# Attention stage: negated logits, second weight parts on VectorE, closer spacing of heads and top-key rounds

## The chip, the cores and the metric

The kernel runs on one core of a Trainium2 chip. A core has TensorE (matmuls and transposes), VectorE, ScalarE and GpSimd (elementwise work), and SyncE, which issues most loads. In the profile they are PE (PEld for its weight loads), DVE, ACT, POOL and SP. The metric is the device time of one execution in microseconds; a kernel's time is the median of its runs.

## The reference, cut to what matters

Two transformer blocks run one after the other on 512 tokens of width 1024. The change lies in the attention of the second block, which has two branches of eight heads (64 wide, two key and value heads each). In the first branch an indexer scores all causal keys, and each query keeps its 128 best (`topk = min(256, 512 // 4)`); the softmax runs over these. In the second branch a query sees a window of 128 keys, and a learned number per head, the sink, joins the softmax's denominator.

```python
# first branch, per block of 128 queries
score = einsum('bqhk,bqh->bqk', relu(s), wb);  score = where(causal, score, -inf)
_, sel = lax.top_k(score, topk)
logits = einsum('bqgrd,bqkgd->bqgrk', qg, ks) * scale
p = softmax(where(valid, logits, -inf));  o = einsum('bqgrk,bqkgd->bqgrd', p, vs)
# second branch, blocks of 128 queries x 256 keys
logits = where(mask, einsum('bnqgrd,bnkgd->bngrqk', qb, kb) * HEAD_DIM ** -0.5, -inf)
p = softmax(concatenate([logits, sink], -1))[..., :-1]
o = einsum('bngrqk,bnkgd->bnqgrd', p, vb)
# both: mix = sigmoid(g_a) * (o_a @ w_branch_a) + sigmoid(g_b) * (o_b @ w_branch_b)
```

## The kernel before

Activations stay in SBUF, weights stream from memory. Each fp32 factor of a dense product is held as a first part (rounded, `hi`) and a second part (the rest, `lo`), and `mm` (line 243) issues three matmuls per block: first x first, first x second, second x first. The stream (`Stream`, line 187) works on a fixed list of units (`plan`). For a unit of up to 128x1024 numbers SyncE loads the raw weights (line 197, three raw buffers), ScalarE writes the first part (line 220, `advance`) and another engine subtracts to get the second part (line 208, `flush`). That engine is `W.eng`, VectorE by default; three units (`ON_POOL`) are always GpSimd's. Before the change line 1165 sets `W.eng` to GpSimd ahead of the projection of the second branch's queries, and line 1253 sets it back behind `w_out_2`. `advance` runs on about every half tick and first flushes the second parts of the first parts issued earlier; each flush also issues the loads that now have a buffer (`pump`).

Everything that is not dense work is written as generators, woven into the dense matmuls by a counter (`Weave`, line 61). A tick is one dense unit of eight K blocks and 128 output features; a projection calls the counter at quarter or half ticks, and a task that yields 0.75 goes on 0.75 ticks later. The order thus made is the program order of every engine's queue, and each engine executes its queue in order. `finish` (line 100) turns the counter with no dense work in between, until the named tasks are done.

In the stage of the change the dense projections come in this order: indexer queries and keys, `bq`, `bk` (second branch), `aq` (4 ticks), `ak` (2), the gate of the second branch (8, line 1204), the branch projection `w_branch_b_2` (4), the gate of the first branch (8, line 1216), `w_branch_a_2` (line 1236), `w_out_2`. Woven into them are: the indexer (line 1015), then 16 rounds of top-key search for each of three query blocks (`top_keys`, line 1035, one round each `TOP_EVERY` ticks), which overwrite the kept scores and make a mask of them; 16 pairs of sliding-window heads, one started each `SWA_EVERY` ticks (line 1176), finished by line 1205; and 16 pairs of first-branch heads, one each `ATT_EVERY` ticks (line 1207), finished by line 1217, where a query block starts only when its keys are known.

One pair of heads (`attend`, line 1045) runs thus: TensorE makes logits (line 1012); VectorE adds the mask and takes the row maximum in one instruction (line 1065), joins the sink (`mx`, line 1068, second branch only) and negates (`nm`, line 1070); ScalarE exponentiates with `nm` as bias and sums (line 1073). Half a tick later VectorE adds the sink's share (`sums`, line 1081) and takes reciprocals (1083), ScalarE scales the weights (1085); 0.75 ticks later TensorE transposes them (1094) and ScalarE copies them out (1096); 0.75 ticks later TensorE multiplies with the values (1103). At the end of each gate ScalarE copies the last block and applies the sigmoid to four blocks at once (line 1200), with a table load of its own. In the branch projection behind the first branch, line 1226 multiplies on VectorE, line 1227 adds on GpSimd, and `split` (line 145) makes the parts `mh` on ScalarE and `ml` on VectorE (line 148).

Of the kernel before, what the change touches and what calls it, by code (L numbers as in the profile page):

```python
# [7 lines left out]
F32 = mybir.dt.float32  # L8
F32R = mybir.dt.float32r
AF = mybir.ActivationFunctionType  # L10
ALU = mybir.AluOpType
# [3 lines left out]
P = 128  # L15
# [6 lines left out]
NEG = -3.0e38  # L22
CUT = -3.2e38
GONE = -3.4e38
MASKED = -1.0e30
NB_RAW = 3
NB_SPLIT = 5
LEAD = 3
LAG_N, LAG_T, LAG_V, LAG_Q, LAG_S = 0.5, 0.75, 0.75, 1, 0.5
SPREAD_Q = 0.25  # L30
SWA_EVERY = 0.75
ON_POOL = (0, 228, 229)
RET_LAG, RET_EVERY = 1, 2
TOP_EVERY = 0.45
ATT_EVERY = 0.7

COLS = [
    ("sgu_ln_g", 8), ("sgu_ln_b", 8),
# [22 lines left out]
class Weave:  # L61
# [13 lines left out]
    def run(self, gen):  # L75

        t = self.spawn(gen)
        self._step(t)
        if not self.inside:
            t["cd"] += self.cur  # L80
        return t
# [26 lines left out]
def tile_kernel(  # L108
# [7 lines left out]
    nc = tc.nc  # L116
    ctx.enter_context(tc.manual_schedule())
    const = ctx.enter_context(tc.tile_pool(name="const", bufs=1))
# [11 lines left out]
    def bigt(shape, name, dt=F32):  # L130
        return big.tile(shape, dt, tag="big", name=name)
# [4 lines left out]
    def tmp2(shape, name, dt=F32):  # L136
        return tp2.tile(shape, dt, tag="t2", name=name)
# [4 lines left out]
    def sm(w, name):  # L142
        return small.tile([P, 16], F32, tag="sm", name=name)[:, :w]
# [93 lines left out]
    W = Stream()  # L237
# [155 lines left out]
    run = wv.run  # L393
# [26 lines left out]
    sinkb = const.tile([P, 8], F32, name="sinkb")  # L420
# [299 lines left out]
    for c in range(2):  # L720
        dense_b(b_units(w_in, 1024 + c * 512), hT,
                lambda t, q, c=c: nc.scalar.activation(
                    v[t // 2][:, t % 2, c * 512:(c + 1) * 512], q, AF.Copy))
# [210 lines left out]
    nc.gpsimd.memset(band, 0.0)  # L934
    nc.gpsimd.affine_select(band, band, [[-1, 256]], ALU.is_ge, MASKED, 128, 1)
    nc.gpsimd.affine_select(band, band, [[1, 256]], ALU.is_gt, MASKED, 0, -1)

    wk_t = bigt([P, 2048], "work")
    work = wk_t[:, 0:1152]
    vb = wk_t[:, 1152:1664].rearrange("p (t c) -> p t c", t=NT)  # L940
# [12 lines left out]
    def q_rope(q, t, name, dst, scale, h0=0):  # L953
        n = 4 * len(dst)
        if (name, t // 2) not in parts:
            parts[name, t // 2] = bigt([P, 2, 8, 2, 64], "hl", F32R)
        hl = parts[name, t // 2][:, t % 2, h0:h0 + n]
        tb = tmp2([P, n, 2, 32], "rq2")
        cos, sin = cs(t)
        rope(q, tb, n, 32, cos, sin)  # L960
        tb = tb.rearrange("p h s c -> p h (s c)")
        yield LAG_S
        split(hl[:, :, 0, :], hl[:, :, 1, :], tb)
        yield LAG_Q + SPREAD_Q * t
        for i, d in enumerate(dst):
            q2 = ps()
            transposes(q2, hl[:, i * 4:i * 4 + 4].bitcast(F32).rearrange("p h s c -> p (h s c)"), 4)
            nc.scalar.activation(
                d[:, :, t * P:(t + 1) * P], q2.rearrange("p (a b) -> p a b", a=4), AF.Copy, scale=scale)
# [65 lines left out]
    def top_keys(t):  # L1035
        wk = work[:, woff[t]:woff[t] + (t + 1) * P]
        for rnd in range(16):
            m8 = sm(8, "m8")
            nc.vector.max(m8, wk)
            nc.vector.match_replace(wk, m8, wk, GONE)  # L1040
            yield TOP_EVERY
        nc.vector.tensor_scalar(wk, wk, CUT, MASKED, op0=ALU.is_gt, op1=ALU.mult)
        kept.add(t)

    def attend(br, t, j, put):

        g = j // 2
        qT, kT = ((aqT, akT), (bqT, bkT))[br]
        k0 = 0 if br == 0 else max(0, t - 1)
        nk = t + 1 - k0  # L1050
        n = nk * P
        if br == 0:
            mask = band[:, P:] if t == 0 else work[:, woff[t]:woff[t] + n]
        else:
            mask = band[:, 256 - n:]
        if n > 256:
            pr = [tmp2([P, T], "pr") for _ in range(2)]
        else:
            pp_ = tmp2([P, 2, 256], "pr")
            pr = [pp_[:, i, :] for i in range(2)]  # L1060
        mx = sm(2, "mx")
        for i in range(2):
            q = ps()
            scores(q, qT, 2 * j + i, t, (kT[0][:, g], kT[1][:, g]), k0 * P, n)
            nc.vector.tensor_tensor_reduce(
                pr[i][:, :n], q[:, :n], mask, 1.0, -3.0e38, ALU.add, ALU.max, mx[:, i:i + 1])
        if br == 1:
            nc.vector.tensor_tensor(mx, mx, sinkb[:, 2 * j:2 * j + 2], ALU.max)
        nm = sm(2, "nm")
        nc.vector.tensor_scalar(nm, mx, -1.0, None, op0=ALU.mult)  # L1070
        sums = sm(2, "sums")
        for i in range(2):
            nc.scalar.activation(pr[i][:, :n], pr[i][:, :n], AF.Exp, bias=nm[:, i:i + 1],  # L1073
                                 accum_out=sums[:, i:i + 1])
        if br == 1:
            es = sm(2, "es")
            nc.vector.tensor_tensor(es, sinkb[:, 2 * j:2 * j + 2], nm, ALU.add)
            nc.scalar.activation(es, es, AF.Exp)
        yield LAG_N
        if br == 1:  # L1080
            nc.vector.tensor_tensor(sums, sums, es, ALU.add)  # L1081
        rs = sm(2, "rs")
        nc.vector.reciprocal(rs, sums)
        for i in range(2):
            nc.scalar.activation(pr[i][:, :n], pr[i][:, :n], AF.Copy, scale=rs[:, i:i + 1])
        yield LAG_T
        pT = {}
        for b0 in range(0, nk, 2):
            nb = min(2, nk - b0)
            q = ps()  # L1090
            for b in range(nb):
                for i in range(2):
                    s = (b * 2 + i) * P
                    nc.tensor.transpose(q[:, s:s + P], pr[i][:, (b0 + b) * P:(b0 + b + 1) * P], ident)  # L1094
            o = tmp2([P, 2, 2, P], "pT")
            nc.scalar.activation(o[:, :nb].rearrange("p b i t -> p (b i t)"), q[:, :nb * 2 * P], AF.Copy)
            for b in range(nb):
                pT[b0 + b] = o[:, b]
        yield LAG_V
        q = ps()  # L1100
        for b in range(nk):
            for i in range(2):
                nc.tensor.matmul(q[i * 64:(i + 1) * 64, :P], vab[br][:, k0 + b, g * 64:(g + 1) * 64],  # L1103
                                 pT[b][:, i, :], start=(b == 0), stop=(b == nk - 1))
        put(j, t * P, (t + 1) * P, q[:, :P])
# [21 lines left out]
    done = {"iq": [], "ik": [], "bq": [], "bk": [], "aq": [], "ak": []}  # L1127
# [22 lines left out]
    bqT = q_tiles("bqT")  # L1150
# [5 lines left out]
    def index_all():  # L1156
# [4 lines left out]
        for t in range(1, NT):  # L1161
            yield from top_keys(t)

    idx_task = wv.spawn(index_all())
    W.eng = nc.gpsimd
    dense_bs([(b_units(w_in_2, 1352),
               lambda t, q: done["bq"].append(run(q_rope(q, t, "bq", bqT, 0.125))))],
             hT2, [(0, 1), (2, 3)])
    dense_bs([(b_units(w_in_2, 1864, 256),
               lambda t, q: done["bk"].append(run(kv(q, t, bkT, vab[1]))))],  # L1170
# [1 line left out]
    aqT = q_tiles("aqT")  # L1172
    akT = k_tiles(gpool, "g", "akT")
    wv.finish(done["bk"])
    ob = Branch()
    swa = wv.spawn(stagger(
        [attend(1, t, j, lambda j, a, b, q: split(ob.hi[:, j, a:b], ob.lo[:, j, a:b], q))
         for j in range(4) for t in range(NT)], SWA_EVERY))
    dense_bs([(b_units(w_in_2, 0),
               lambda t, q: done["aq"].append(run(q_rope(q, t, "aq", aqT, 0.125))))],  # L1180
             hT2, [(0, 1), (2, 3)])
    dense_bs([(b_units(w_in_2, 512, 256),
               lambda t, q: done["ak"].append(run(kv(q, t, akT, vab[0]))))],
# [66 lines left out]
            norms.append(run(norm_T(t, xrow(t), g_mlp, h3T)))  # L1250

    down(w_out_2, KD, mix_pair, fin)
    W.eng = nc.vector

    u2 = []

# [81 lines left out]
```

## Time and profile before

| | before |
|---|---|
| median of 3 runs | 1616.56 us (1616.42 to 1617.55) |
| profiled execution, its own time | 1612.59 us |
| its span, first to last instruction | 1610.8 us |
| TensorE busy, mean granted clock | 98%, 0.994 |
| VectorE, ScalarE, GpSimd busy | 47%, 38%, 20% |

The page gives busy time and a chain of waits for the whole span; TensorE is 82% of the chain. The page's slices show where VectorE is fullest: between about 890 and 1130 us, the stage described above, its tenths are 7 and 8, against 2 to 6 nearly everywhere else. The stage is then read in windows and in the timeline. A wait in the waits view names the instruction that ended it, which may itself have waited for another. A group's mean duration contains any time in which the instruction had been started but was held.

### The profile page before, as it was taken

The page shows a single profiled execution, that of the slowest core. Times are in us where ns is not written, and L with a number is a line of the kernel's source. Part 1 is how long each engine was busy: PE and PEld are TensorE (multiplying, and loading weights), DVE is VectorE, ACT ScalarE, POOL GpSimd, SP SyncE. Part 2 cuts the span into 40 slices and gives each one's busy share as a digit, 9 for nine tenths or more (in the row PEclk, how much of TensorE's full clock was granted, in tenths as well). Part 3 has the DMA queues.
Part 4 walks back from the last instruction along what each step waited for, and adds up shares of the span by engine and source line. Part 5 has one row for each costly group of instructions (what it writes and reads, how often), then busy time and mean ns, then how long its engine had stood idle before and what let it go on. Part 6 is the DMA issues. An engine that isn't in the chain of part 4 may idle for free.

```text
span 1610.8 us, 19774 instructions
## 1 busy us (share of the span) xinstructions
PE 1577.0 (98%) x7844; PEld 1320.0 (82%) x7844; DVE 763.1 (47%) x1309; ACT 613.3 (38%) x1012; POOL 329.8 (20%) x300
## 2 busy tenths in 40 slices
PE   9999999999999999999998999999999999999998
PEld 8888888888888888888887888777877988878886
DVE  4247323453546544455336788778443322233333
ACT  5232223322324433334324456665833323233222
POOL 1015000341004122111005444232345211010000
PEclk9999999999999999999999999999999999999999
DMA  6332333212441233334331421222133333232221
GB/s 204 98 92 71 100 105 92 79 53 90 146 129 55 82 102 92 104 91 146 105 95 49 143 61 49 76 69 76 53 131 92 92 105 103 82 119 96 99 92 52
DMA packets 187247, 151.75 MB, mean 94 GB/s; under 512 B 5218, under 2 KB 157410, under 8 KB 186644
## 3 DMA queue, kind: packets, MB, share of 16 engines
q1 hardware_dynamic: 185072, 144.01, 29.8%
q0 software_dynamic: 1504, 5.44, 1.0%
q8 instruction: 61, 1.00, 0.2%
q10 hardware_dynamic: 580, 1.05, 0.2%
q14 instruction: 30, 0.25, 0.0%
HBM read 146.29 MB, written 4.19 MB: 93 GB/s over the span
## 4 chain that ended last, share of the span: by engine, by line
PE 82%; DVE 8%; ACT 4%; POOL 2%; issue 2%; DMA 0%; POOLq 0%; DVEq 0%; ACTq 0%
PE ps L246 25%; PE ps L247 25%; PE ps L245 25%; PE ps L279 1%; ACT pr L1073 1%; DVE work L1029 1%; PE ps L1012 1%; PE ps L1103 1%; PE ps L1094 1%; PE ps L772 1%; POOL Ya L1227 1%; DVE sums L1081 1%; ACT wh L220 1%; POOL rstd L460 1%; PE ps L487 1%
## 5 line engine op out<-in xcount | busy, mean ns | idle before, releaser
L220 ACT ACTIVATE wh<-wr 128x1024 fp32r<-128x1024 f32 (+1 forms) x259 | 270.9, 1051 | 251.3 <-PE ps L247 119.2
L208 DVE TENSOR_TENSOR wl<-wr,wh 128x1024 fp32r<-128x1024 f32 (+1 forms) x212 | 257.6, 1226 | 172.3 <-ACT wh L220 172.3
L245 PE MATMUL ps<-wh,ls 128*128 128x512 f32 x432 | 168.4, 390 | 1.2 <-ACT ls L147 1.2
L247 PE MATMUL ps<-wh,ls 128*128 128x512 f32 x432 | 168.2, 389 | 0.3 <-DVE ls L148 0.3
L246 PE MATMUL ps<-wl,ls 128*128 128x512 f32 x432 | 168.1, 389 | 0.0
L208 POOL TENSOR_TENSOR wl<-wr,wh 128x1024 fp32r<-128x1024 f32 x47 | 114.5, 2444 | 134.9 <-ACT wh L220 134.8
L245 PE MATMUL ps<-h2Th,wh 128*128 128x512 f32 (+1 forms) x352 | 133.5, 379 | 0.0
L246 PE MATMUL ps<-h2Tl,wh 128*128 128x512 f32 (+1 forms) x352 | 133.5, 379 | 0.0
L247 PE MATMUL ps<-h2Th,wl 128*128 128x512 f32 (+1 forms) x352 | 133.5, 379 | 0.0
L245 PE MATMUL ps<-hTh,wh 128*128 128x512 f32 (+1 forms) x256 | 97.7, 382 | 0.0
L247 PE MATMUL ps<-hTh,wl 128*128 128x512 f32 (+1 forms) x256 | 96.4, 376 | 0.0
L246 PE MATMUL ps<-hTl,wh 128*128 128x512 f32 (+1 forms) x256 | 96.2, 376 | 0.0
L245 PEld LDWEIGHTS ps<-wh,ls 128*128 128x128 f32 x432 | 81.1, 188 | 18.5 <-ACT ls L147 1.6
L245 PE MATMUL ps<-h3Th,wh 128*128 128x512 f32 (+1 forms) x256 | 96.2, 376 | 0.0
L246 PE MATMUL ps<-h3Tl,wh 128*128 128x512 f32 (+1 forms) x256 | 96.2, 376 | 0.0
L247 PE MATMUL ps<-h3Th,wl 128*128 128x512 f32 (+1 forms) x256 | 96.2, 376 | 0.0
L247 PEld LDWEIGHTS ps<-wh,ls 128*128 128x128 f32 x432 | 81.1, 188 | 17.6 <-DVE ls L148 0.8
L246 PEld LDWEIGHTS ps<-wl,ls 128*128 128x128 f32 x432 | 81.1, 188 | 16.7
L896 ACT ACTIVATE hid<-ps,cols 128x512 f32<-128x512 f32 x44 | 34.3, 780 | 144.8 <-PE ps L247 144.8
L897 DVE SCALAR_TENSOR_TENSOR hid<-ps,cols,hid 128x511 f32<-128x511 f32 x44 | 33.0, 749 | 116.8 <-ACT hid L896 116.8
L904 POOL TENSOR_TENSOR act<-hid 128x512 f32<-128x512 f32 x22 | 45.2, 2055 | 194.1 <-DVE hid L899 180.1
L246 PEld LDWEIGHTS ps<-h2Tl,wh 128*128 128x128 f32 x352 | 66.2, 188 | 12.5
(312 smaller groups left out, 3283.4 us busy)
## 6 DMA issues: line engine op xcount, KB each, us to landing
wr<-in_w_in_dram SPq DMA_DIRECT2D x86, 512.0 KB, 3.8
wr<-in_w_up_dram SPq DMA_DIRECT2D x76, 512.0 KB, 3.9
wr<-in_w_down_dram SPq DMA_DIRECT2D x54, 512.0 KB, 3.7
wr<-in_w_out_dram SPq DMA_DIRECT2D x16, 512.0 KB, 3.9
wr<-in_w_sgu_o_dram SPq DMA_DIRECT2D x8, 512.0 KB, 4.2
wr<-in_w_ret_o_dram SPq DMA_DIRECT2D x8, 512.0 KB, 4.3
g<-in_rows_dram POOLq DMA_DIRECT2D x6, 512.0 KB, 7.2
x<-in_x_dram SPq DMA_DIRECT2D x4, 512.0 KB, 5.7
```

The lines of the kernel that those rows point to most:

```text
L208: eng.tensor_tensor(lo, self.raw.pop(i), hi.bitcast(F32), ALU.subtract)
L220: nc.scalar.activation(hi, self.raw[self.n_hi], AF.Copy)
L245: nc.tensor.matmul(q, lhs[0], rhs[0], start=start, stop=False)
L246: nc.tensor.matmul(q, lhs[0], rhs[1], start=False, stop=False)
L247: nc.tensor.matmul(q, lhs[1], rhs[0], start=False, stop=stop)
L279: nc.tensor.matmul(q[:, :256], wslice(u, k, 0, P)[i], act.at(k, 0, 256)[j], start=(i + j + k == 0), stop=(i == 1 and k == K - 1))
L460: nc.gpsimd.tensor_tensor(r, r, nhalf, ALU.pow)
L487: nc.tensor.transpose(q[:, i * P:(i + 1) * P], xn[:, k * P:(k + 1) * P], ident)
L772: nc.tensor.matmul(o, kz[:, d, c - d, :], vc[c], start=True, stop=True)
L896: nc.scalar.activation(o, q, AF.Identity, bias=col("conv_b", f), scale=col("conv_w1", f))
L897: nc.vector.scalar_tensor_tensor(o[:, 1:], q[:, :T - 1], col("conv_w0", f), o[:, 1:], ALU.mult, ALU.add)
L904: nc.gpsimd.tensor_tensor(act[fa // 4][:, fa % 4, :], a, b, ALU.mult)
```

## The change

The logits are made negative: the query copies carry -0.125 in place of 0.125, masked places get +1e30 in place of -1e30, the fused instruction takes the minimum in place of the maximum, and the exponential gets a scale of -1. What was `nm` (minus the maximum) is then the minimum itself, so the negation per pair of heads is left out; the sink joins by a minimum with a negated copy, `nsink`, made once. The two lines that hand the second parts of the weights to GpSimd in this stage and back are left out, so VectorE makes them. Three spacings become smaller.

```diff
-MASKED = -1.0e30
+MASKED = 1.0e30
...
-SWA_EVERY = 0.75
+SWA_EVERY = 0.65
...
-TOP_EVERY = 0.45
-ATT_EVERY = 0.7
+TOP_EVERY = 0.38
+ATT_EVERY = 0.6
...
+    nsink = const.tile([P, 8], F32, name="nsink")
+    nc.vector.tensor_scalar(nsink, sinkb, -1.0, None, op0=ALU.mult)
...
-        mx = sm(2, "mx")
+        nm = sm(2, "nm")
...
             nc.vector.tensor_tensor_reduce(
-                pr[i][:, :n], q[:, :n], mask, 1.0, -3.0e38, ALU.add, ALU.max, mx[:, i:i + 1])
+                pr[i][:, :n], q[:, :n], mask, 1.0, 3.0e38, ALU.add, ALU.min, nm[:, i:i + 1])
         if br == 1:
-            nc.vector.tensor_tensor(mx, mx, sinkb[:, 2 * j:2 * j + 2], ALU.max)
-        nm = sm(2, "nm")
-        nc.vector.tensor_scalar(nm, mx, -1.0, None, op0=ALU.mult)
+            nc.vector.tensor_tensor(nm, nm, nsink[:, 2 * j:2 * j + 2], ALU.min)
         sums = sm(2, "sums")
         for i in range(2):
-            nc.scalar.activation(pr[i][:, :n], pr[i][:, :n], AF.Exp, bias=nm[:, i:i + 1],
+            nc.scalar.activation(pr[i][:, :n], pr[i][:, :n], AF.Exp, bias=nm[:, i:i + 1], scale=-1.0,
                                  accum_out=sums[:, i:i + 1])
...
-    W.eng = nc.gpsimd
     dense_bs([(b_units(w_in_2, 1352),
-               lambda t, q: done["bq"].append(run(q_rope(q, t, "bq", bqT, 0.125))))],
+               lambda t, q: done["bq"].append(run(q_rope(q, t, "bq", bqT, -0.125))))],
...
-               lambda t, q: done["aq"].append(run(q_rope(q, t, "aq", aqT, 0.125))))],
+               lambda t, q: done["aq"].append(run(q_rope(q, t, "aq", aqT, -0.125))))],
...
     down(w_out_2, KD, mix_pair, fin)
-    W.eng = nc.vector
```

## Rows read from the trace of the kernel before

**Rows 1.** Waits of TensorE, 880 to 1215 us: total, times, longest.

```profile
PE ps L1094 <- ACT pr L1085: 3.8, 3, 3.1
PE ps L1103 <- ACT pT L1096: 3.5, 3, 2.3
PE ps L493 <- ACT pT L1096: 2.2, 1, 2.2
PE ps L246 <- POOL wl L208: 1.8, 1, 1.8
PE ps L493 <- DVE hl L148: 0.8, 1, 0.8
```

**Rows 2.** Busy us by stretch: PE, PEld, DVE, ACT, POOL, granted clock, DMA, GB/s.

```profile
950.00:970.00 20.00, 16.81 (x83) 13.51 (x82) 16.05 (x44) 14.17 (x34) 4.50 (x4) 0.95 0.16 46
970.00:990.00 20.00, 20.00 (x117) 16.11 (x116) 17.59 (x50) 11.89 (x35) 9.09 (x6) 0.97 0.24 57
1170.00:1190.00 20.00, 17.39 (x76) 13.69 (x75) 7.48 (x10) 7.46 (x11) 5.72 (x4) 0.83 0.47 169
1210.00:1240.00 30.00, 28.19 (x121) 22.90 (x120) 7.32 (x8) 9.80 (x12) 17.98 (x10) 0.94 0.42 123
```

**Rows 3.** Groups of VectorE and GpSimd, 880 to 1215 us: busy, mean ns, idle.

```profile
L1070 DVE TENSOR_SCALAR nm<-mx 128x2 f32<-128x2 f32 x32 | 19.1, 596 | 1.1
L1081 DVE TENSOR_TENSOR sums<-sums,es 128x2 f32<-128x2 f32 x16 | 11.3, 704 | 0.0
L1068 DVE TENSOR_TENSOR mx<-mx,sinkb 128x2 f32<-128x2 f32 x16 | 5.5, 346 | 0.6
L148 DVE TENSOR_TENSOR ml<-Ya,mh 128x512 fp32r<-128x512 f32 x8 | 11.6, 1445 | 16.5 <-ACT mh L147 16.5
...
L208 POOL TENSOR_TENSOR wl<-wr,wh 128x1024 fp32r<-128x1024 f32 x37 | 89.7, 2429 | 132.0 <-ACT wh L220 132.0
```

**Rows 4.** The page, costliest groups: the second parts that VectorE makes.

```profile
L208 DVE TENSOR_TENSOR wl<-wr,wh 128x1024 fp32r<-128x1024 f32 (+1 forms) x212 | 257.6, 1226 | 172.3 <-ACT wh L220 172.3
```

**Rows 5.** Timeline, GpSimd and VectorE: a long nm and a plain one.

```profile
1002.38 4.72 POOL L208 TENSOR_TENSOR wl<-wr,wh 128x1024 fp32r<-128x1024 f32 x2
...
1004.83 2.31 DVE L1070 TENSOR_SCALAR nm<-mx 128x2 f32<-128x2 f32 x1
...
1057.21 0.17 DVE L1070 TENSOR_SCALAR nm<-mx 128x2 f32<-128x2 f32 x1
```

**Rows 6.** Timeline around the first sliding-window head: GpSimd, VectorE, TensorE.

```profile
961.57 2.40 POOL L208 TENSOR_TENSOR wl<-wr,wh 128x1024 fp32r<-128x1024 f32 x1 [10.18 <-ACT wh L220]
...
962.01 3.37 DVE L1029 SCALAR_TENSOR_TENSOR work<-relu,work 128x512 f32<-128x512 f32 x2 [2.27 <-ACT relu L1023]
...
968.02 0.77 PE L1094 MATMUL ps<-ident,pr 128*128 128x128 f32 x2 [3.06 <-ACT pr L1085]
```

**Rows 7.** Timeline at the end of the last gate projection: TensorE, ScalarE.

```profile
1168.17 1.09 PE L1103 MATMUL ps<-pT,va 128*64 128x128 f32 x16
1169.20 1.09 PE L1094 MATMUL ps<-ident,pr 128*128 128x128 f32 x8
...
1174.54 0.80 PE L245 MATMUL ps<-obh,wh 128*128 128x512 f32 x1
...
1170.19 1.91 ACT L1200 ACTIVATE Ya<-Ya 128x2048 f32<-128x2048 f32 x1
```

**Rows 8.** Timeline of the branch projection: ml plain and long, and TensorE.

```profile
1191.19 0.69 DVE L148 TENSOR_TENSOR ml<-Ya,mh 128x512 fp32r<-128x512 f32 x1 [2.06 <-ACT mh L147]
...
1210.99 2.18 DVE L148 TENSOR_TENSOR ml<-Ya,mh 128x512 fp32r<-128x512 f32 x1 [2.06 <-ACT mh L147]
...
1212.67 0.50 PE L246 MATMUL ps<-wl,mh 128*128 128x512 f32 x1 [1.81 <-POOL wl L208]
```

**Rows 9.** Timeline of GpSimd where VectorE still makes the second parts.

```profile
899.44 0.86 POOL L510 TENSOR_TENSOR rq<-rope 128x256 f32<-128x256 f32 x1 [2.83 <-DVE rope L504]
900.57 1.57 POOL L510 TENSOR_TENSOR rq<-rope 128x256 f32<-128x256 f32 x1 [0.28 <-DVE rope L504]
```

## The prediction

> **What bounds it now.** I read the page's first two parts, then TensorE's waits, then the windows with the clock, then VectorE's groups with their mean durations, and last the timeline around each wait. TensorE is busy for 98% of the span, so only the time in which it stands or runs at the lower clock can be won; the change leaves its matmuls as they are. In the stretch of the change (880 to 1215 us) the waits view lists few idle stretches [rows 1]: 3.8 us of softmax transposes on the scaled weights, 3.5 us of value matmuls on the transposed weights (2.3 of it one wait at the very end), 2.2 us of key transposes, 1.8 us on a second part made by GpSimd, 0.8 us on a rotated query: 12.1 us in all. After the longer ones the granted clock falls to its lower level for a while; one minus the granted clock, times the window, gives 1.0 and 0.6 us after the first head, 3.4 us at the end of attention, 1.8 us in the projection behind it [rows 2]: 6.8 us. So 18.9 us, 1.2%, is about what can be had. Gaps too short for the waits view come on top.
>
> Who makes TensorE wait is seen one step back. VectorE's `nm`, on two numbers per partition, takes 0.17 us when left alone [rows 5] and 596 ns on average; `sums` averages 704 ns and `mx` 346 ns [rows 3]. In the timeline an `nm` begins at 1004.83 and ends at 1007.14, just when a pair of GpSimd's second parts ends (1002.38 plus 4.72) [rows 5]. So a small VectorE operation that falls on one of GpSimd's 37 second parts (2429 ns each [rows 3]) is held until that ends, and behind it stand the exponential on ScalarE, the reciprocal, the scaling and the transposes.
>
> **Part 1: second parts from GpSimd to VectorE.** Off GpSimd go 37 x 2.43 = 90 us; VectorE gains 37 x 1.226 = 45.4 us [rows 3, 4]. It loses the holds: 32 x (596 - 170) ns = 13.6 us on `nm`, 16 x (704 - 170) = 8.5 on `sums`, 16 x (346 - 170) = 2.8 on `mx`, 8 x (1445 - 690) = 6.0 on `ml` [rows 3, 5, 8], 30.9 us. With part 2 (5.4 us) that is 36.3 against 45.4: VectorE gets up to 9 us more work, nearer none because other lines, not shown, stretch too. The gain is not less work but its shape: 1.2 us at a fixed place in the queue in place of up to 2.3 us in the middle of a softmax. Term by term:
> - First sliding-window head: TensorE waits 3.06 us until 968.02 for weights that stand behind an indexer product held from 962.01 to the end of GpSimd's part, 961.57 + 2.40 = 963.97 [rows 6], 1.96 us. The second part whose first half was made just before now comes half a tick later, behind the head's reciprocal. Gain 1.9 us, and with a wait of 1.1 us left I take 1.2 of the 1.6 us of low clock [rows 2].
> - Key transposes, 2.2 us [rows 1]: the hold of 2.14 us goes, a second part of 1.23 may stand in its place. Gain 0.9 to 2.1, taken 1.2, nearer the end at which one still stands there.
> - The shorter waits on the scaled and the transposed weights, 3.8 + 3.5 - 3.1 - 2.3 = 1.9 us [rows 1]. Some come behind ScalarE's sigmoid with its table loads, which stays. Gain 0 to 1.9, taken 1.0. The rotated query: 0.8 us, gain 0.5.
> - Branch projection after attention. VectorE's order per feature block is product, then `ml` after GpSimd's sum and ScalarE's copy. Every second `ml` is held, 2.18 against 0.69 us [rows 8]; now a second part of 1.23 us follows it instead, so a pair of blocks gets 0.26 us shorter, 0.8 us by the last block. The part on which TensorE waits until 1212.67 [rows 8] then ends at about 1210.99 - 0.8 + 0.69 + 1.23 = 1212.1 (1210.99 is the start of the last `ml`, after three such pairs). Gain 0.5; the lower clock behind it stays.
> - Loads: SyncE issues the next weight load when a second part is done. On VectorE that is about half a tick later than on GpSimd; three raw buffers and one unit a tick cover it, and ScalarE's waits name no load between 900 and 1170 us. Nothing; without that cover, half a tick for each late unit, about 4 us (some 25 ticks fill the 200 us from 968.02 [rows 6] to 1168.17 [rows 7]).
> - GpSimd's own sums (24 rotary, 8 in the branch projection). The trace shows the hold in the other direction as well: a rotary sum took 1.57 us against 0.86 while VectorE made second parts [rows 9]. Behind each rotary sum lies half a tick or more. In the branch projection VectorE reaches a second part only after `ml`, so after the sum that `ml` waits for. Nothing taken; if all four second parts there fell on a sum, 4 x 1.23 = 4.9 us (rival 2).
>
> The Trainium skill, SBUF — State Buffer, Who interferes with whom, says that GpSimd and a VectorE instruction with two SBUF inputs exclude each other for a whole instruction, whichever starts first, and that issue order decides who loses; the new second parts are of that kind, so this speaks against the change. The trace agrees in both directions (2.31 against 0.17 us, 1.57 against 0.86); by that rule alone, with the second parts starting first, the forecast would lose the 4.9 us, by the order of the queues it loses none.
>
> **Part 2: negated logits.** 32 `nm` go, at 0.17 us left alone [rows 5]: 5.4 us of VectorE, and one link of the chain in each head. Minimum for maximum, a negative scale on ScalarE and in the query copy, and the other mask are the same instructions with other constants. One product on eight numbers is added ahead of the stage, beside the end of the norm. Counted above.
>
> **Part 3: spacing.** A tick is one gate unit (8 x 3 matmuls). Behind the start of the sliding-window heads lie 4 + 2 + 8 = 14 ticks; they need 15 x 0.75 + 2 = 13.25, then 15 x 0.65 + 2 = 11.75. Behind the start of the second heads lie 4 + 8 = 12; they need 15 x 0.7 + 2 = 12.5, then 11. The top-key rounds need 48 x 0.45 = 21.6, then 18.2. So before, the last heads run past the end of the dense work; after, nothing does. But that end is held by ScalarE anyhow: dense work stops at 1168.17, the sigmoid ends at 1170.19 + 1.91 = 1172.10, the branch projection starts at 1174.54 [rows 7], 6.4 us later, and in between TensorE does two heads' value matmuls and one set of transposes, 1.03 us each [rows 7]. After the change those 3.0 us lie before, and TensorE then stands empty through copy, table load and sigmoid (3.9 us) and one split copy (a quarter of the sigmoid's width, 0.5 at least, 0.6 taken): 3.0 + 4.5 = 7.5 against 6.4. Loss 1.0 (0 to 1.5); the low clock stays (3.4 us [rows 2]).
> Denser heads cost no work, but a tick holds 1/0.65 in place of 1/0.75 heads and 2.6 in place of 2.2 rounds, while VectorE is already busy 16 to 17.6 of 20 us where the query projection runs [rows 2]. Unknown, 8 us either way (the 8.0 us of waits that rival 1 adds up, gone or doubled); taken as nothing, because the holds leave as the density comes.
>
> **Sum.** 1.9 + 1.2 + 1.2 + 1.0 + 0.5 + 0.5 - 1.0 = 5.3 us. On the profiled execution (1612.59 us, span 1610.8) that is 1607.3; the median shown, 1616.56, stands 4.0 above that execution, and I carry the difference over: 1611.3.
>
> **Rivals.**
> 1. More goes. If every wait of [rows 1] before the end goes (3.8 + 1.2 + 2.2 + 0.8 = 8.0) with the low clock behind the first head and the branch projection (1.6 + 1.8), less 1.0, plus 0.5: 10.9 us, 1605.7; with the end's low clock also gone, 1602.3. For it: nearly all waits lead back to held operations. Against: second parts take 1.2 us at the same places.
> 2. The holds change sides, or re-form. VectorE's work is the same, closer packed, and its second parts now hold GpSimd's sums in the branch projection: 1611.3 + 4.9 = 1616.2. Or only the first head's 1.9 + 1.2 us are won and 1.0 lost at the end: 1614.5. Between them 1615.5. For it: VectorE's total is no lower. Against: the order of VectorE's queue in the branch projection.
> 3. Slower. A second part on VectorE must wait for ScalarE's first part, and VectorE executes in order, so the next head's masked sum and reciprocal queue behind it; on GpSimd only second parts queued. Elsewhere VectorE idles 172.3 us before 212 of them, 0.8 us each [rows 4]. 37 x 0.8 = 30 us; if a third reaches TensorE, 10 - 5.3 = 5 us slower: 1621.3. It decides from the point at which ScalarE runs more than the half tick between first and second part behind VectorE, most likely after a sigmoid. Against: VectorE waits for ScalarE in every head anyway.
>
> **How the numbers follow.** Forecast 50%, more 16%, re-formed 22%, slower 12%. The range, 1602.5 to 1618.5, takes in rival 1, rival 2 and the bounds down to a loss of 2 us, and leaves out most of rival 3. Faster by over 0.2% (3.2 us, about what a measurement of this kernel can tell from no change) is forecast and rival 1, 66%; same 22%; slower 12%.
>
> **What would show it.** `sums` and the sink minimum near 0.17 us on average; no second part on GpSimd but the three fixed ones; the first head's wait near 1 us and no low clock behind it; the waits on scaled weights halved; an idle stretch of over 4 us on TensorE before the branch projection, ended by ScalarE. Wrong if VectorE idles on ScalarE's first parts (rival 3), or if short gaps grow between 970 and 1070 us (rival 2).

## The result and the profile after

| | before | after |
|---|---|---|
| median of 7 runs each | 1616.36 us (1612.60 to 1617.55) | 1622.82 us (1621.44 to 1626.34) |
| ratio, 95% interval | | 1.0054 [1.0041, 1.0066] |
| profiled execution, its span | 1612.59, 1610.8 us | 1626.34, 1624.5 us |

The change makes the kernel 0.54% slower, where 5 us faster was forecast; the time lies outside the range. In the profiled executions the stage, from the first matmul of the indexer queries to the first of `w_out_2`, takes 327.9 us before and 337.9 after. The rest of their difference lies ahead of the stage, where the two kernels do the same work but for one product on eight numbers, and where executions differ by up to 4.5 us; stretches of the stage are therefore compared below by their own lengths. Of the kernel before one of the fastest executions was profiled, of the kernel after the slowest, so these 10.0 us need not agree with the 6.5 between the medians.

The page of the kernel after, busy time of each engine and the group of VectorE's second parts (busy, mean ns of one, idle before them):

```profile
PE 1585.6 (98%) x7844; PEld 1326.8 (82%) x7844; DVE 764.4 (47%) x1322; ACT 610.6 (38%) x1010; POOL 224.3 (14%) x256
...
L208 DVE TENSOR_TENSOR wl<-wr,wh 128x1024 fp32r<-128x1024 f32 x256 | 310.9, 1225 | 183.8 <-ACT wh L220 183.7
```

Groups of VectorE in the stage, kernel after:

```profile
L148 DVE TENSOR_TENSOR ml<-Ya,mh 128x512 fp32r<-128x512 f32 x8 | 5.5, 692 | 16.6 <-ACT mh L147 16.6
...
L1071 DVE TENSOR_TENSOR nm<-nm,nsink 128x2 f32<-128x2 f32 x16 | 3.2, 199 | 0.6
...
L1082 DVE TENSOR_TENSOR sums<-sums,es 128x2 f32<-128x2 f32 x16 | 3.0, 185 | 0.0
```

The holds of [rows 3, 5] are gone as foretold: 185 in place of 704 ns on `sums`, 199 in place of 346 on the sink's instruction, 692 in place of 1445 on `ml`. VectorE's total is what it was (764.4 against 763.1 us), with 44 more second parts in it (212 before, [rows 4]; seven of them lie behind the 1215 us where the prediction's count of 37 ended). So the loss is not work. Waits of TensorE, 880 to 1235 us, kernel after (total, times, longest):

```profile
PE ps L245 <- ACT obh L147: 4.4, 1, 4.4
PE ps L246 <- DVE wl L208: 4.1, 3, 1.8
PE ps L245 <- DVE rope L504: 2.9, 2, 1.6
PE ps L1095 <- ACT pr L1086: 2.6, 1, 2.6
...
PE ps L1104 <- ACT pT L1097: 2.0, 2, 1.0
PE ps L493 <- DVE nm L1068: 1.1, 1, 1.1
PE ps L1104 <- DVE rope L504: 1.0, 1, 1.0
PE ps L493 <- ACT pT L1097: 0.9, 1, 0.9
PE ps L1095 <- DVE rope L504: 0.6, 1, 0.6
PE ps L493 <- DVE obl L148: 0.4, 1, 0.4
```

Against [rows 1], the 3.06 us of the first head are gone, and new names stand behind the arrow: `rope`, `nm`, `obl`. None of these is an operand of the waiting matmul. PSUM is the memory that TensorE writes its results to, and the kernel has 8 tiles of it (`ps`). All three instructions read such a tile, so TensorE has caught up with a late VectorE and waits until the tile that it is about to write has been read. Where this happens is read from windows (busy us of PE, PEld, DVE, ACT, POOL, granted clock, DMA, GB/s), kernel after: the stretch of the `aq` and `ak` projections, then two windows with a low clock.

```profile
958.95:1020.30 61.35, 52.47 (x341) 43.73 (x340) 45.61 (x160) 35.19 (x101) 8.15 (x8) 0.97 0.20 52
1010.00:1030.00 20.00, 15.68 (x86) 12.26 (x85) 13.54 (x57) 10.38 (x35) 3.04 (x3) 0.74 0.21 53
1180.00:1200.00 20.00, 15.57 (x57) 12.01 (x56) 4.52 (x8) 8.09 (x10) 2.57 (x2) 0.83 0.34 132
```

The length of each stretch in the profiled executions, between the first matmuls of the projections in the timeline (us):

| kernel | iq to bk | aq | ak | gate b | branch b | gate a and end | branch a |
|---|---|---|---|---|---|---|---|
| before | 83.0 | 35.9 | 19.4 | 63.3 | 27.2 | 74.7 | 24.5 |
| after | 84.2 | 35.7 | 25.7 | 63.8 | 28.9 | 75.0 | 24.6 |
| e2, second parts only | 82.9 | 31.8 | 19.3 | 60.0 | 27.2 | 73.8 | 25.6 |
| e4, old spacing | 82.9 | 31.2 | 18.4 | 59.9 | 27.1 | 74.7 | 24.3 |
| e5, e4 with closer heads b | 82.7 | 36.3 | 25.1 | 60.9 | 27.1 | 73.9 | 23.9 |
| e7, e4 with closer heads a | 82.9 | 31.3 | 18.4 | 59.9 | 28.7 | 72.6 | 22.4 |
| e8, after with starts last | 84.1 | 34.3 | 23.2 | 61.6 | 28.7 | 75.0 | 24.2 |
| e9, after with shared PSUM | 82.7 | 35.1 | 23.9 | 67.7 | 28.9 | 75.0 | 24.8 |
| e11, e8 and e9 together | 84.2 | 33.6 | 21.4 | 60.6 | 28.7 | 75.0 | 24.4 |
| e13, e4 with late value step | 84.1 | 31.9 | 21.9 | 61.0 | 27.1 | 73.9 | 24.3 |
| e16, after with old spacing b | 82.9 | 31.8 | 18.5 | 60.6 | 28.9 | 75.0 | 24.3 |

Before against after, only `ak` has clearly grown, by 6.3 us, which hides two things: parts 1 and 2 took 5.7 us out of `aq` and `ak` (e4), and the spacing put 11.7 us back, and 3.9 into the gate behind them. The first column, whose stretch no spacing reaches, shows how far equal stretches differ: 82.7 to 84.2 us. In branch b the kernels with 0.6 for the first branch's heads take at least 1.6 us more: 12 more of the heads' matmuls fall into it (56 in place of 44), which the gate behind it then lacks (248 in place of 260).

### The profile page after: what moved, and what is told of

Read it like the earlier page. It is cut to its first block, busy times and chain, and to the rows that moved or that the text cites. A ratio compares the mean times of both kernels' runs of the same rounds, so it can differ in the third digit from the quotient of the medians.

```text
span 1624.5 us, 19720 instructions
## 1 busy us (share of the span) xinstructions
PE 1585.6 (98%) x7844; PEld 1326.8 (82%) x7844; DVE 764.4 (47%) x1322; ACT 610.6 (38%) x1010; POOL 224.3 (14%) x256
## 4 chain that ended last, share of the span: by engine, by line
PE 84%; DVE 7%; ACT 4%; POOL 2%; issue 2%; DMA 0%; DVEq 0%; POOLq 0%; ACTq 0%
PE ps L245 25%; PE ps L246 25%; PE ps L247 25%; PE ps L279 1%; DVE wl L208 1%; PE ps L1014 1%; ACT pr L1074 1%; PE ps L1104 1%; PE ps L487 1%; DVE work L1042 1%; POOL Ya L1227 1%; PE ps L772 1%; PE ps L1095 1%; PE ps L493 1%; DVE pr L1068 1%
## 5 line engine op out<-in xcount | busy, mean ns | idle before, releaser
L208 DVE TENSOR_TENSOR wl<-wr,wh 128x1024 fp32r<-128x1024 f32 x256 | 310.9, 1225 | 183.8 <-ACT wh L220 183.7
L896 ACT ACTIVATE hid<-ps,cols 128x512 f32<-128x512 f32 x44 | 34.3, 780 | 144.9 <-PE ps L247 144.9
L245 PEld LDWEIGHTS ps<-h2Th,wh 128*128 128x128 f32 x352 | 66.2, 188 | 12.6
L247 PEld LDWEIGHTS ps<-h2Th,wl 128*128 128x128 f32 x352 | 66.2, 188 | 12.3
```

The source lines that it names most:

```text
L208: eng.tensor_tensor(lo, self.raw.pop(i), hi.bitcast(F32), ALU.subtract)
L245: nc.tensor.matmul(q, lhs[0], rhs[0], start=start, stop=False)
L247: nc.tensor.matmul(q, lhs[1], rhs[0], start=False, stop=stop)
L896: nc.scalar.activation(o, q, AF.Identity, bias=col("conv_b", f), scale=col("conv_w1", f))
```

## The experiments

Ratios are to the kernel before, run beside each of them.

**One part alone.** Theory A: the spacing costs and the rest gains. B: the second parts in VectorE's queue cost. C: only both together cost. The edits of e1 and e4 are against the changed kernel, those of e2 and e3 against the kernel before.

**e1_negated_only**

```diff
-SWA_EVERY = 0.65
+SWA_EVERY = 0.75
...
-TOP_EVERY = 0.38
-ATT_EVERY = 0.6
+TOP_EVERY = 0.45
+ATT_EVERY = 0.7
...
+    W.eng = nc.gpsimd
...
+    W.eng = nc.vector
```

> The kernel before with the negated logits alone; second parts stay on GpSimd, spacing stays. Theory A (the closer spacing costs, the rest gains) and theory B (second parts in VectorE's queue cost) both expect a small gain: 32 instructions at 596 ns on average go from VectorE, and TensorE's waits of 12.1 us between 880 and 1215 us fall by at most 3, so -1 to -4 us, ratio 0.998 to 0.9995. A ratio above 1.001 would speak for a third thing: that the changed order of VectorE's queue alone moves waits about.

Measured 1611.34 us, 0.9972 [0.9962, 0.9982]. A gain of 4.6 us, slightly above the band: an instruction that took 596 ns on average is gone, and with it the wait of 2.2 us on the key transposes. `sums` is still held (711 ns).

**e2_second_parts_only**

```diff
-    W.eng = nc.gpsimd
...
-    W.eng = nc.vector
```

> The kernel before with only the 37 second parts moved to VectorE. Theory A: the holds go (sums, nm near 0.17 us) and nothing takes their place at this spacing: -3 to -6 us, ratio 0.996 to 0.998, and no low clock near 968 us. Theory B: VectorE carries 9 to 14 us more than in the changed kernel's own balance and its queue makes the softmax late: +4 to +10 us, ratio 1.003 to 1.006, with low clock between 970 and 1030 us as in the changed kernel (10.2 us from 1016). Theory C (only both together cost): 0.998 to 1.000.

Measured 1605.06 us, 0.9938 [0.9926, 0.9951]: a gain of 10.9 us by the medians, about twice the band of theory A (7.4 in the stage by the profiled executions). B falls: the part that the prediction's slower rival blamed is the best part of the change. `nm` averages 174 and `sums` 219 ns.

**e3_spacing_only**

```diff
-SWA_EVERY = 0.75
+SWA_EVERY = 0.65
...
-TOP_EVERY = 0.45
-ATT_EVERY = 0.7
+TOP_EVERY = 0.38
+ATT_EVERY = 0.6
```

> The kernel before with only the three closer spacings; the holds by GpSimd stay. Theory A: all of the loss and more, +6 to +14 us, ratio 1.004 to 1.009, the stretch from the end of the bk projection to the gate of the second branch longer by 6 us or more. Theory B: +1 us at the end of attention and nothing else, ratio 0.999 to 1.001. Theory C: 0.999 to 1.002.

Measured 1635.54 us, 1.0127 [1.0113, 1.0141], 19.6 us slower, above the band of theory A (6 to 14 us); C falls too. In this kernel `sums` averages 185 ns, and the sink's instruction 608, although GpSimd still makes the second parts: a hold depends on where an instruction falls, and the spacing alone moves that.

**e4_old_spacing**

```diff
-SWA_EVERY = 0.65
+SWA_EVERY = 0.75
...
-TOP_EVERY = 0.38
-ATT_EVERY = 0.6
+TOP_EVERY = 0.45
+ATT_EVERY = 0.7
```

> The changed kernel with the three old spacings: negated logits and second parts on VectorE. Theory A: the forecast's gain without the forecast's loss at the end, -4 to -8 us, ratio 0.995 to 0.9975. Theory B: the loss stays, +5 to +10 us, ratio 1.003 to 1.006, with the low clock near 1016 us. Theory C: 0.997 to 0.9995.

Measured 1605.42 us, 0.9943 [0.9930, 0.9956], and no low clock between 960 and 1160 us. Theory A holds, with larger sizes: parts 1 and 2 gain 10.5 us, the spacing costs 17.4. With the second parts moved, the negation brings nothing more (e2 against e4).

**One spacing at a time**, on e4.

**e5_heads_b_closer**

```diff
-SWA_EVERY = 0.75
+SWA_EVERY = 0.65
```

> From here on the base is e4_old_spacing (negated logits, second parts on VectorE, old spacings: 1605.4 us, 17 us under the changed kernel), and one spacing is made closer at a time. Here the sliding-window heads: 0.65 in place of 0.75 ticks. If it is these heads (the stretch from the end of the bk projection to the gate grew from 49.6 us in e4 to 61.4 in the changed kernel): 1615 to 1622 us, ratio to before 0.999 to 1.004, and the low clock near 1016 us comes back. If it is the top-key rounds or the sum of all three: 1605 to 1609 us, ratio 0.993 to 0.996.

Measured 1618.51 us, 1.0023 [1.0013, 1.0032]: 13.1 us more than e4, 11.7 of them in `aq` and `ak`, with the low clock at their end.

**e6_top_keys_closer**

```diff
-TOP_EVERY = 0.45
+TOP_EVERY = 0.38
```

> e4_old_spacing with the top-key rounds alone closer, 0.38 in place of 0.45 ticks. If VectorE's load counts (2.6 in place of 2.2 rounds a tick, beside the query projection where it is fullest): 1610 to 1618 us, ratio 0.996 to 1.001. If the heads of the second branch count: 1604 to 1608 us, ratio 0.9925 to 0.995.

Measured 1606.94 us, 0.9954 [0.9939, 0.9969], not to be told from e4. VectorE's load by rounds is not the cause.

**e7_heads_a_closer**

```diff
-ATT_EVERY = 0.7
+ATT_EVERY = 0.6
```

> e4_old_spacing with the first branch's heads alone closer, 0.6 in place of 0.7 ticks. The prediction's step for the end of attention (all heads done before the dense work ends, TensorE then idle behind the sigmoid) gives +1.0, 0 to +1.5 us: 1605 to 1607 us. The wait of 4.4 us on the first branch's split copy is then there as in the changed kernel. If the 12 ticks with denser heads cost as the second branch's do: 1610 to 1618 us.

Measured 1602.08 us, 0.9929 [0.9913, 0.9945], the fastest kernel of all, 13 us under before. Its interval overlaps that of e4. Its end is 4.1 us shorter (the last two columns of the table), of which 1.6 is work moved into branch b. The wait on the split copy is 2.5 us, not the 4.4 expected. What is won over e4 is not a wait but the clock: TensorE's longest wait at the end and the window around it, for e4, e6 and e7.

```profile
PE ps L1104 <- ACT pT L1097: 2.3, 1, 2.3
1160.00:1190.00 30.00, 27.39 (x149) 21.96 (x146) 11.06 (x18) 12.47 (x17) 5.15 (x4) 0.89 0.27 105
```

```profile
PE ps L245 <- ACT obh L147: 2.5, 1, 2.5
1160.00:1190.00 30.00, 27.24 (x141) 22.06 (x140) 10.99 (x17) 13.43 (x18) 5.15 (x4) 0.94 0.27 106
```

```profile
PE ps L245 <- ACT obh L147: 2.5, 1, 2.5
1160.00:1190.00 30.00, 27.25 (x147) 22.25 (x146) 12.46 (x19) 12.97 (x17) 6.42 (x5) 1.00 0.34 123
```

A wait as long or shorter is followed by a lower clock in the first two and not in the third; why is not shown. No step of the expectation foresaw that.

**Why closer heads cost.** The window of the `aq` and `ak` projections in e4, beside the first of the three windows of the kernel after, holds the clue:

```profile
958.12:1007.76 49.64, 48.68 (x326) 41.72 (x324) 41.34 (x142) 32.61 (x91) 7.59 (x7) 1.00 0.22 55
```

In the kernel after VectorE does 4.3 us more in this stretch (45.61 against 41.34) but needs 11.7 us longer; it idles 15.7 us where it idled 8.3. An engine that stands more while its work is late waits for somebody. Not all of the 11.7 us is waiting: of TensorE's matmuls beside the dense ones, 146 in place of 130 fall into this stretch, and 130 in place of 146 into the gate behind it. By branch b, where 12 take 1.6 us, these 16 are about 2 us, an estimate. Waits of VectorE and ScalarE in that stretch, kernel after, then e4:

```profile
DVE obl L148 <- ACT obh L147: 7.0, 5, 2.3
...
ACT pr L1074 <- DVE nm L1071: 18.7, 9, 3.8
```

```profile
DVE obl L148 <- ACT obh L147: 1.3, 1, 1.3
...
ACT pr L1074 <- DVE nm L1071: 9.1, 6, 2.2
```

The timeline of the kernel after, just ahead of its low clock, shows why the two wait for each other:

```profile
1013.16 0.28 DVE L1068 CUSTOM_DVE_ANT_0 pr<-ps,band 128x128 f32<-128x128 f32 x1
...
1013.51 1.09 PE L493 MATMUL ps<-ident,hl 128*128 128x128 f32 x8 [1.06 <-DVE nm L1068]
...
1013.95 0.40 ACT L1074 ACTIVATE pr<-pr,nm 128x128 f32<-128x128 f32 x1 [3.76 <-DVE nm L1071]
...
1014.83 0.25 ACT L147 ACTIVATE obh<-ps 128x128 fp32r<-128x128 f32 x1
1014.99 0.58 ACT L1097 ACTIVATE pT<-ps 128x512 f32<-128x512 f32 x1
1015.12 0.29 DVE L148 TENSOR_TENSOR obl<-ps,obh 128x128 fp32r<-128x128 f32 x1 [1.06 <-ACT obh L147]
...
1015.51 0.17 DVE L1084 RECIPROCAL rs<-sums 128x2 f32<-128x2 f32 x1
...
1015.62 0.73 PE L1104 MATMUL ps<-pT,work 128*64 128x128 f32 x8 [1.02 <-ACT pT L1097]
```

One quarter tick holds the start of a new head and, behind it, the value step and the transposes of older ones. ScalarE stands 3.76 us before the new head's exponential, which wants `nm`. Behind it in ScalarE's queue are the first part of an older head's output (`obh`) and the copy `pT`, which want nothing of the new head. VectorE then stands 1.06 us for that `obh`, with the next reciprocal behind it, and TensorE 1.02 us for `pT`. By the order written out, a start has a quarter tick without other steps of heads in 13 of 16 cases at 0.75 ticks and in 1 of 16 at 0.65; it shares one with a value step in 1 and in 9 cases. At 0.75, three quarter ticks, the later steps (0.5, 1.25 and 2.0 ticks after a start) all fall two quarters behind a start; at 0.65 they beat against the starts. Theory O: that order costs. Theory D: the density itself. Theory P: the 8 PSUM tiles go round too fast.

**e8_start_last**

```diff
-        for t in list(self.tasks):
+        for t in sorted(self.tasks, key=lambda t: "late" in t):
...
+    swa["late"] = True
...
+    att["late"] = True
```

> The changed kernel with all its spacings, with one thing turned about: where a head's start falls into the same quarter tick as later steps of earlier heads, the start comes behind them in every queue, not ahead. By the order written out, 9 of the 16 starts in the second branch share a quarter tick with the value step of an earlier head at 0.65 ticks, and 1 of 16 at 0.75. Theory O (order: in such a quarter VectorE's second part of the output waits for ScalarE's first part, which stands behind the new head's exponentials, which wait for VectorE's minimum): VectorE's waits on ScalarE's first part of the output (30.4 us in 15 waits in the changed kernel) fall to under 15 us and half or more of the 17 us comes back: 1606 to 1614 us, ratio 0.994 to 0.9985. Theory D (density: more work per tick than VectorE or ScalarE can do, whatever its order): 1619 to 1625 us, ratio 1.002 to 1.0055.

Measured 1617.19 us, 1.0017 [1.0008, 1.0027]: 5.6 us come back, a third, less than O expected and more than D. In `aq` and `ak` VectorE's wait on `obh` falls from 7.0 to 1.7 us and ScalarE's on `nm` from 18.7 to 6.9; but ScalarE's on the reciprocal, 6.6 in the kernel after, rises to 14.3, so part of the exchange has only moved. Waits of ScalarE, VectorE and TensorE there:

```profile
ACT pr L1086 <- DVE rs L1084: 14.3, 8, 3.1
ACT pr L1074 <- DVE nm L1071: 6.9, 6, 1.6
...
DVE obl L148 <- ACT obh L147: 1.7, 3, 0.9
...
PE ps L245 <- ACT aqT L970: 3.4, 2, 2.0
PE ps L1014 <- DVE rope L504: 0.9, 1, 0.9
PE ps L1095 <- ACT pr L1086: 0.5, 1, 0.5
PE ps L245 <- DVE rope L504: 0.5, 1, 0.5
```

**e9_shared_bank**

```diff
-        for i in range(2):
-            q = ps()
-            scores(q, qT, ...)
+        q = ps()
+        qs = [q, ps()] if n > 256 else [q[:, :256], q[:, 256:]]
+        for i in range(2):
+            scores(qs[i], qT, ...)
+        for i in range(2):
             nc.vector.tensor_tensor_reduce(
-                pr[i][:, :n], q[:, :n], mask, ...)
+                pr[i][:, :n], qs[i][:, :n], mask, ...)
```

> The changed kernel with all its spacings and its order of heads, but a pair of heads whose logits are at most 256 wide writes them into the two halves of one PSUM tile in place of two tiles; no instruction goes or comes. The kernel has 8 PSUM tiles that go round. In the order of the instructions as written, the median distance from the last read of a tile to its next write, in the aq and ak projections, is 15 dense matmuls in the kernel before, 10.5 in e4_old_spacing, 6 in the changed kernel and e5_heads_b_closer, and 11 here. Theory P (PSUM: closer heads use up the round of tiles, TensorE waits until a late VectorE or ScalarE has read one): a good part of the 17 us against e4 comes back, 1606 to 1615 us, ratio 0.994 to 0.9995, and TensorE's waits on rope, nm and obl between the bk projection and the gate (3.9 us in the changed kernel) go to under 1 us. Theory O (order of steps inside a quarter tick) alone: 1618 to 1625 us, ratio 1.002 to 1.0055. Theory D (too much work per tick): the same.

Measured 1625.03 us, 1.0069 [1.0057, 1.0082]. P falls as a cause by itself. The waits on PSUM tiles went as expected, and others took their place; waits of TensorE in `aq` and `ak`:

```profile
PE ps L1106 <- ACT pT L1099: 5.8, 3, 3.3
PE ps L493 <- ACT pT L1099: 0.5, 1, 0.5
PE ps L1106 <- DVE obl L148: 0.4, 1, 0.4
PE ps L1097 <- DVE rope L504: 0.4, 1, 0.4
```

TensorE gets past the tile and then waits for the transposed weights. VectorE's waits on `obh` (7.0 us) and ScalarE's on `nm` (18.7) are those of the kernel after. PSUM is where the lateness shows, not where it arises. `aq` and `ak` got 2.4 us shorter and the gate 3.8 longer.

**e10_seven_banks**

```diff
+    pin = ps()
+    nc.vector.memset(pin[:, 0:1], 0.0)
...
+    nc.vector.tensor_copy(sm(1, "pin"), pin[:, 0:1])
```

> e4_old_spacing (1605.4 us) with one of the 8 PSUM tiles kept occupied from the start of the sliding-window heads to their end: one number is written at the start and read at the end. Spacing and order are the old ones; the median distance from last read to next write falls from 10.5 to 8 dense matmuls in aq and ak. Theory P: +3 to +12 us, 1608 to 1617 us, with waits of TensorE on rope, nm or obl that e4 doesn't have. Theories O and D: 1604 to 1607 us.

Measured 1607.17 us, 0.9956 [0.9943, 0.9968], not to be told from e4: against P again.

**e11_shared_start_last**

The edits of e8 and e9 together.

> e8_start_last (closer spacings, starts behind the later steps of earlier heads: 1617.2 us) with the logits of a pair in one PSUM tile; median distance 12 in place of 7 dense matmuls. If order and PSUM are two causes that add: 1603 to 1611 us, ratio 0.993 to 0.998, below e9. If they are one cause seen twice (a late reader matters only because its tile is wanted): within 3 us of e9. Theory D: 1614 to 1620 us.

Measured 1612.45 us, 0.9994 [0.9985, 1.0003], 4.7 us under e8 and 12.6 under e9, though slower than the band for two causes that add. Sharing tiles helps once the order is turned, when the PSUM tiles are what TensorE waits for. `aq` and `ak` are still 5.3 us longer than in e4, of which some 2 us are the heads' matmuls that closer heads bring there.

**e12_shared_old_b**

The edit of e9 on e7.

> e7_heads_a_closer (old spacings but 0.6 for the first branch's heads, the fastest so far: 1602.1 us) with the logits of a pair in one PSUM tile; median distance 14 in place of 10.5 dense matmuls. Theory P: the few waits left (0.3 us on rope, 0.5 us on the scaled weights) and short gaps shrink, -0 to -4 us: 1598 to 1602.5 us, ratio 0.990 to 0.993. A second head's logits written while VectorE still reads the first half could cost instead; then over 1604 us.

Measured 1602.89 us, 0.9934 [0.9921, 0.9946], no difference from e7.

**e13_value_at_start**

```diff
-        yield LAG_V
+        yield LAG_V + 0.25 * br
```

> e4_old_spacing (1605.4 us; heads each 0.75 ticks) with the value step of the second branch's heads a quarter tick later, so that it falls into the quarter tick of a later head's start, behind that start in the queues: by the order as written 12 of the 16 starts share it with a value step, 1 of 16 in e4, 9 of 16 in the changed kernel. Work per tick stays. Theory O (order): VectorE's waits on ScalarE's first part of the output between the bk projection and the gate rise from 1.3 us to 5 us or more, and the time by 3 to 10 us: 1608 to 1615 us. Theory D (density alone): 1604 to 1607 us.

Measured 1610.29 us, 0.9967 [0.9956, 0.9979]: 4.9 us slower than e4 with no head closer and no work added. Waits in `aq` and `ak`:

```profile
ACT pr L1086 <- DVE rs L1084: 9.7, 5, 2.8
...
DVE obl L148 <- ACT obh L147: 7.0, 5, 2.1
...
PE ps L1095 <- ACT pr L1086: 2.5, 2, 2.3
```

VectorE's wait on `obh` is 7.0 us in 5 waits, as in the kernel after (1.3 in e4), and TensorE waits for scaled weights behind it. This is the plainest evidence for O. (One PSUM tile fewer at the old spacing, e10, moved nothing.)

**e14_a_closer_start_last**

The edit of e8 on e7.

> e7_heads_a_closer (1602.1 us) with the starts behind the later steps of earlier heads, as in e8_start_last. In the second branch 13 of 16 starts stand alone in their quarter tick there, so little can change; the first branch's starts at 0.6 ticks often share one. Theory O: 0 to -3 us, 1599 to 1602.5 us. Theory D: 1601.5 to 1603 us.

Measured 1605.29 us, 0.9939 [0.9928, 0.9951], a miss: 3.2 us above e7, though the intervals overlap. `ak` takes 21.7 in place of 18.4 us, with a wait of 2.1 us on the scaled weights and a low clock. Branch a takes 1.6 us more as well: the clock fell behind the same wait of 2.5 us that left it up in e7. The edit also puts a start behind the steps of the `aq` and `ak` tiles, which stood behind it before. Starts last is no rule; where starts stand alone it delays them for nothing.

**e15_closer_from_ninth**

```diff
-            yield every
+            yield every if i < 8 or every != SWA_EVERY else 0.65
```

> e4_old_spacing with the second branch's heads closer (0.65 ticks) from the ninth on only: the first eight, which start beside the aq and ak projections, keep 0.75. If closer heads cost only where VectorE and ScalarE also turn the queries and keys of the first branch: 1604 to 1607 us. If they cost wherever starts and later steps share a quarter tick (4 of the 7 starts in the gate do so here, none in e4): 1608 to 1613 us.

Measured 1607.05 us, 0.9950 [0.9935, 0.9966], not to be told from e4. Crowding beside the gate alone, where no queries and keys are turned, costs little; the gate takes 61.8 in place of 59.9 us. As only seven starts are closer there, that the place decides is argued rather than shown.

**e16_old_b_only**

```diff
-SWA_EVERY = 0.65
+SWA_EVERY = 0.75
```

> The changed kernel with the sliding-window heads back at 0.75 ticks; top-key rounds at 0.38 and the first branch's heads at 0.6 stay. If the other 6 us come from the end of attention (the last block's keys are known 3.5 ticks earlier at 0.38, so its heads, at 0.6, end before the dense work does): 1606 to 1609.5 us, the wait of 4.4 us on the first branch's split copy as in the changed kernel, against 2.5 us in e7_heads_a_closer, and low clock behind it. If they come from the sliding-window heads and the rounds together: 1602 to 1605 us and a wait near 2.5 us.

Measured 1610.18 us, 0.9969 [0.9956, 0.9982], a little above the band of the first case. The wait is 4.4 us, and the end is 4.4 us longer than in e7. The window at the end of attention, as shown for the others under e7:

```profile
1160.00:1190.00 30.00, 25.57 (x106) 20.21 (x103) 9.87 (x15) 11.14 (x14) 5.15 (x4) 0.89 0.32 116
```

With the rounds at 0.45 the last block's keys come late, its heads still run while ScalarE works on the sigmoid, and TensorE stands 2.5 us. At 0.38 beside 0.6 they are through earlier, it stands 4.4 us, and the clock falls; with 0.38 alone (e6) it stands 2.5. So the 17.4 us between e4 and the changed kernel are -3.3 for the first branch's heads (e7), 8.1 for the rounds beside them (e16, 4.4 of it at this end, the rest within the scatter of the two medians) and 12.6 for the second branch's heads.

## Why the prediction was wrong

- **The step that failed** is the last of part 3: denser heads were "unknown, 8 us either way" and "taken as nothing, because the holds leave as the density comes". The second branch's heads alone cost 13.1 us (e5), outside those bounds. The bound was made from the waits that the kernel before already had, doubled or gone; a closer spacing made waits of a kind that it did not have. The holds had indeed left, in e4, and that did not pay for it. The spacing was reckoned as heads per tick, while the order written out, which could be read ahead, showed starts and later steps falling into the same quarter tick (1 of 16 starts alone in place of 13). e13 shows that crowding costs at an unchanged density, e8 that turning the order gives a third back, and e15 that beside the gate alone it costs little. Of the 5.3 us that e11 keeps in `aq` and `ak`, some 2 are work that comes earlier; how much of the rest is density itself stays open.
- **Part 1** was right in its mechanism and too small. Its terms add up to 6.3 us (1.9 + 1.2 + 1.2 + 1.0 + 0.5 + 0.5); e2 gained 10.9 by the medians, 7.4 in the stage by the profiled executions. In the stretches of the table, `aq` (first head and the low clock behind it) gave 4.1 us where 3.1 was taken, and the gate 3.3 where 1.0 was taken for all shorter waits. `ak` gave 0.1: the wait on the key transposes left, for which 1.2 was taken, but one of 1.1 us on scaled weights came. Loads at nothing held. GpSimd's own sums were nearly untouched: the rotary sums of the queries average 1137 ns in e2 against 1135 before, the sums of the branch projection 1289 against 1288. Those of the keys were held in the new direction, 1028 ns on average against 816, but no wait of TensorE names them. The Trainium skill, SBUF — State Buffer, Who interferes with whom, was weighed there as speaking against this part. The holds that it describes are in the traces, though `nm`, quoted there at 2.31 against 0.17 us, has only one SBUF input; `sums` with two, 704 against 219 ns in e2, is the fitting pair. In e2 those on GpSimd's sums do not show in TensorE's waits.
- **Part 2** is worth 4.6 us only while GpSimd still holds the instruction (e1), and nothing after part 1 (e2 against e4). Counting it within part 1 was right.
- **The end of attention.** The idle stretch was put at 4.5 us and is 4.4; the loss was put at 1.0. The two last columns give 0.5, but with the work that the closer heads moved into branch b the three last give about 2. What was missed is that with 0.6 alone, without 0.38, the last block's keys hold its heads back to where TensorE would be empty: the three columns are then some 2.5 us shorter than in e4 (e7), which had a low clock there where e7 had none.
- **Branch projection.** Its wait went from 1.8 us on GpSimd's to 1.5 on VectorE's second part, a gain of 0.3 against 0.5.
- **The rivals.** Rival 3 gave 1621.3 us, near the 1622.82 measured, by luck: e2 refutes its mechanism, and in the kernel after VectorE waits only 5.5 us on ScalarE's first parts of weights between 900 and 1190 us. Its form was right for another pair: VectorE, in order, stands for ScalarE's first part of the *output*, 22.1 us in the second branch against 12.6 in the kernel before. Rival 2 named the sign to look for, short gaps between 970 and 1070 us, and they grew, but no hold by GpSimd's second parts made them: the three that GpSimd still makes lie outside that stretch.
- **A sum of the prediction.** Its 12.1 us of waits "in all" leave out lines of the same view: 1.6 us on a second part made by VectorE in the indexer's projection, ahead of the change, and 1.2 us of short ones; all of them are 14.9. No term of the sum rests on these.

## What to carry to other kernels

Where work is woven into a stream by a counter, a spacing sets not only how many tasks run per tick but which of their steps meet in one slot; write the slots out before changing it, and choose a spacing that puts the start of one task and the late steps of others apart (here three quarters of a tick did, 0.65 did not). An engine that gets idler while its consumers wait longer may be in an exchange with another in-order engine; freeing buffers then only moved the wait here (e9). Parts of a change that gain and lose hide each other: parts 1 and 2 with the closer heads of the first branch alone run in 1602.1 us, 20.7 under the change as a whole.

## What the runs showed of the hardware

The length of a wait of TensorE alone did not decide whether the granted clock fell. At the end of attention one of 2.5 us went with a clock of 1.00 over 30 us (e7), another of 2.5 us with 0.94 (e6), and one of 2.3 us (e4) and one of 4.4 us (e16) both with 0.89. In the kernel after it also fell, to 0.74 over 1010 to 1030 us, behind a run of waits of about 1 us each, the longest of them 1.2. And the time from the start of the program to the stage differed between executions by up to 4.5 us (its first matmul at 870.9 to 875.4 us) in kernels that are the same up to there, as much as many of the effects looked for.
